# RWKV-7 and pooling trunk: the chunk solves take both heads through one block-diagonal operand, with right-hand sides of 64 columns

## The chip, the cores and the metric

The program runs on one core of a Trainium2 chip. The metric is the device time of one execution in microseconds (us); lower is better. A core has a matrix engine (PE, with its weight loads shown apart as PEld), a vector engine (DVE), a scalar engine (ACT), a general engine (POOL) and queues that issue DMAs (SP among them). Each engine takes its instructions in order.

## The reference

The model has one layer (DEPTH = 1), T = 512 tokens, D = 2048. The part that matters here is the RWKV-7 group: 16 heads of 64 channels, each with a state S of 64x64 that is updated token by token:

```python
h = rms_norm(x, norm_g[i])
z = h @ w_in[i]          # r, k, v, decay, rate | rwkv gate | pool input | pool gate
# per head, per token t:
sa = S @ (-kk_t)
S  = S * w_t + sa (kk_t * a_t)^T + v_t k_t^T
y_t = S @ r_t
```

Beside it stand a pooling group, the gates, an output projection and a last gated embedding; each of these is a dense product with large weights.

## The kernel before

Everything that is dense (the projections `z`, later the output and the gate) is done in three passes on PE (`mm3`), each a 128x512 matmul on operands split into a high and a low part. A weight tile arrives as `raw`, ACT casts it to `whi` (L132), DVE subtracts to get `wlo` (L133).

The recurrence is done in chunks of C = 64 tokens (NCH = 8), for a pair j of heads at a time (NJ = 8 pairs; a pair fills 128 partitions). For each pair:

- `scores(j)` forms the products of keys and rates inside a chunk and masks them into `mt` (L630).
- `invert(j)` inverts the 32x32 triangular blocks row by row on DVE (31 steps, `tm` L657 and `xw` L661), writes the result to memory (`xd`) and loads it as the blocks on the diagonal of `x1`, a tile of 8 units x 64 columns that POOL zeroes for every pair.
- `gather(j)` builds the 32x32 block off the diagonal of each inverse: transposes `y1` on DVE (L734), 16 small matmuls `pq` (L739), copies `q` on ACT (L745), 16 small matmuls `px` (L748), copies into `x1` on ACT (L752).
- `recur(j)` is the chain over the 8 chunks. In each chunk: `py` on PE (the state's part); `zs` on DVE (L787) adds `mv` to it; `pu` on PE (L793) is the solve, the inverse times `zs`; `uv` are two copies on ACT (L797); `ps` on PE is the state's update; `sbd` are two operations on DVE (L807, L809) that write the next state.

Before, `zs` is 128x128 and holds the right-hand sides of both heads side by side in one half of its partitions, zeros in the other. `pu` multiplies by `x1` of both heads (128 columns), so its 128x128 result holds four 64x64 blocks, of which the two on the diagonal are used.

PE takes its instructions in the order of the program. Between the steps of the chain the program pumps filler, matmuls of the dense projections: 6 between `py` and `pu`, 9 between `pu` and `ps`, 9 after `ps` (`HC = (6, 9, 9)`), and others between the bursts of `gather` (`H1 = 6` matmuls each). As long as DVE and ACT are done within this filler, PE does not wait. The order on DVE, ACT, POOL and SP is made by a scheduler at build time from its own estimate of durations; `zs`, `sbd` and `uv` have a raised priority there (`HP`). `step()` lets three rows of the next pair's inversion through after the operation in `lead[0]`.

Of the kernel before, what the change touches and what calls it, by code (L numbers as in the profile page):

```python
# [9 lines left out]
F32 = mybir.dt.float32  # L10
# [3 lines left out]
ALU = mybir.AluOpType  # L14

P = 128
# [5 lines left out]
NJ = DR // P  # L22
LORA = 64
C = 64
# [10 lines left out]
def trunk_kernel(ctx: ExitStack, tc: tile.TileContext, x, p, norm_g, w_in, mu, w0, w_up, a0, a_up,  # L35
# [329 lines left out]
    for t_ in sbd + zsp:  # L365
# [243 lines left out]
    def scores(j):  # L609
        ar, bk, v_ = (st_[j][n_] for n_ in ("ar", "bk", "v_"))  # L610
        kph, kpl = st_[j].pop("kp")

        ps = psM.tile([P, T], F32, name=f"pbo{j}", tag="m")
        mm(ps, blk, kph, start=True, stop=False)
        mm(ps, blk, kpl, start=False, stop=True)
        bv = rw.tile([P, T], F32, name=f"bv{j}", tag="bv", bufs=2)
        nc.vector.tensor_tensor(bv, ps, v_, ALU.mult)

        mt = rw.tile([P, 2, 8, 2, C], F32, name=f"mt{j}", tag="mt", bufs=2)
        pm = [[psM.tile([P, T], F32, name=f"pm{j}_{par}0", tag="m"),  # L620
               psY.tile([P, T], F32, name=f"pm{j}_{par}1", tag="y")] for par in range(2)]
        for par in range(2):
            for q in range(4):
                for h in range(2):
                    rows = slice(64 * h, 64 * h + 64)
                    mm(pm[par][h][:, q * P:(q + 1) * P], bk[rows, q, 2 * par:2 * par + 2, :],
                       ar[rows, q, 2 * par:2 * par + 2, :], start=True, stop=True)
        for par in range(2):
            for h in range(2):
                nc.vector.tensor_tensor(mt[:, par, h::2, :, :],  # L630
                                        pm[par][h].rearrange("p (u a t) -> p u a t", u=4, a=2),
                                        msk[:, par:par + 2, :].unsqueeze(1).to_broadcast([P, 4, 2, C]), ALU.mult)

        nd = dram.tile([2, 2, 8, 32, 32], F32, name=f"nd{j}", tag="nd")
        for par in range(2):
            pb = 64 * (1 - par)
            for b in range(2):
                rows = slice(pb + 32 * b, pb + 32 * b + 32)
                nc.sync.dma_start(out=nd[par, b].rearrange("u r c -> r u c"),
                                  in_=mt[rows, par, :, 1 - par, 32 * b:32 * b + 32])  # L640
        nb = []
        for i in range(2):
            t_ = rw.tile([P, 16, 32], F32, name=f"n32{j}_{i}", tag=("kk", "kp")[i])
            nc.sync.dma_start(out=t_, in_=nd[:, :, :, 16 * i:16 * i + 16, :].rearrange(
                "a b u r c -> (a b u) r c").unsqueeze(0).to_broadcast([4, 32, 16, 32]))
            nb.append(t_)
        st_[j].update(mt=mt, nb=nb, bv=bv)


    def invert(j):  # L650
        nb = st_[j].pop("nb")
        xw = rw.tile([P, 8, 32], F32, name=f"xw{j}", tag="xw")
        tm = rw.tile([P, 8, 32], F32, name=f"tm{j}", tag="tm")
        for s in range(31):
            n_, w_ = s // 4 + 1, 31 - s
            xin = i32 if s == 0 else xw
            nc.vector.tensor_tensor(tm[:, 0:n_, 0:w_], xin[:, 0:n_, s:s + 1].to_broadcast([P, n_, w_]),  # L657
                                    nb[s // 16][:, s % 16:s % 16 + 1, s + 1:32].to_broadcast([P, n_, w_]), ALU.mult)
            if s == 0:
                nc.gpsimd.tensor_copy(xw, i32)  # L660
            nc.vector.tensor_tensor(xw[:, 0:n_, s + 1:32], xw[:, 0:n_, s + 1:32], tm[:, 0:n_, 0:w_], ALU.add)  # L661
            yield
        xd = dram.tile([2, 2, 8, 8, 4, 32], F32, name=f"xd{j}", tag="xd")
        for q in range(4):
            nc.sync.dma_start(out=xd[:, :, :, :, q, :].rearrange("a b u i c -> (a b u) i c"),
                              in_=xw[32 * q:32 * q + 32])
        x1 = rw.tile([P, 8, C], F32, name=f"x1{j}", tag="x1", bufs=2)
        nc.gpsimd.memset(x1, 0.0)
        for par in range(2):
            pb = 64 * (1 - par)  # L670
            for b in range(2):
                nc.sync.dma_start(out=x1[pb + 32 * b:pb + 32 * b + 32, :, 32 * b:32 * b + 32],
                                  in_=xd[par, b].rearrange("u i q c -> (i q) u c"))

        st_[j]["x1"] = x1


    def gather(j):
# [25 lines left out]
        ps = psM.tile([P, 8, C], F32, name=f"pmv{j}", tag="m")  # L704
        for u in range(8):
            for par in range(2):
                pb, kb = 64 * (1 - par), 64 * par
                h = u % 2
                mm(ps[pb:pb + 64, u, :], mt[kb:kb + 64, par, u, 1 - par, :],
                   uv[kb:kb + 64, 2 * (u // 2) + par, 64 * h:64 * h + 64], start=True, stop=True)  # L710
        mv = rw.tile([P, 4, P], F32, name=f"mv{j}", tag="mv")
        nc.scalar.copy(zsp[0][64:128, :].rearrange("p (h t) -> p h t", h=2), ps[64:128, 0:2, :])
        nc.scalar.copy(mv.rearrange("p q (h t) -> p (q h) t", h=2), ps)

        d.update(uv=uv, bkn=bkn, mv=mv)
# [4 lines left out]
            pending.pop()()  # L720
        pump(HX)

        x1 = d["x1"]

        def units(fn):
            for u in range(8):
                for par in range(2):
                    fn(u, par, 64 * (1 - par))

        y1 = rw.tile([P, 8, 32], F32, name=f"y1{j}", tag="tm")  # L730

        with tc.issue_after(late[0].ins):
            for pb in (0, 64):
                yt = nc.vector.transpose(y1[pb:pb + 32], x1[pb:pb + 32, :, 0:32])  # L734
# [4 lines left out]
        units(lambda u, par, pb: mm(ps3[pb + 32:pb + 64, u, :],  # L739
                                                  mt[pb:pb + 32, par, u, 1 - par, 32:64],  # L740
                                                  y1[pb:pb + 32, u, :], start=True, stop=True,
                                                  tile_position=(pb, pb + 32)))
        q2t = rw.tile([P, 8, 32], F32, name=f"q2{j}", tag="xw")
        for pb in (0, 64):
            nc.scalar.copy(q2t[pb + 32:pb + 64], ps3[pb + 32:pb + 64])  # L745
        pump(H1)
        ps4 = psM.tile([P, 8, 32], F32, name=f"px2{j}", tag="m")
        units(lambda u, par, pb: mm(ps4[pb:pb + 32, u, :], q2t[pb + 32:pb + 64, u, :],  # L748
                                                  x1[pb + 32:pb + 64, u, 32:64], start=True, stop=True,
                                                  tile_position=(pb + 32, pb)))  # L750
        for pb in (0, 64):
            nc.scalar.copy(x1[pb:pb + 32, :, 32:64], ps4[pb:pb + 32])  # L752
        pump(H1)


    def recur(j, work, between):
        d = st_.pop(j)
        pw, ar, mt, bv, uv, bkn, mv, x1 = (d[n_] for n_ in ("pw", "ar", "mt", "bv", "uv", "bkn", "mv", "x1"))
        hop = [0]
        HC1, HC2, HC3 = HC  # L760
        lead = [None]
# [12 lines left out]
        for ch in range(NCH):  # L774
# [8 lines left out]
            if ch > 0:  # L783
                mm(py[:, sl], ar[:, q, 2 * par:2 * par + 2, :], cur, start=ch in (1, 4), stop=True,
                                 skip_group_check=True)
                with tc.high_priority(offset=HP):
                    lead[0] = nc.vector.tensor_tensor(zs[pb:pb + 64], py[pb:pb + 64, sl], mv[pb:pb + 64, q, :],  # L787
                                                      ALU.add)
                step()
                pump(HC1)  # L790

            psu = psS.tile([P, T], F32, name=f"pu{j}_{ch}", tag="s")
            mm(psu[:, 0:P], x1[:, 2 * q:2 * q + 2, :], zs, start=True, stop=True)  # L793
            for h in range(2):
                hc = slice(64 * h, 64 * h + 64)
                with tc.high_priority(offset=HP):
                    nc.scalar.copy(uv[pb:pb + 64, ch, hc], psu[hc, hc])  # L797
            step()
            pump(HC2)
            if ch < NCH - 1:  # L800
# [16 lines left out]
            if ch % 4 == 3:  # L817
                for qq in range(2):
                    for h in range(2):
                        for pr in range(2):  # L820
                            c_ = ch - 3 + 2 * qq + pr
                            yr = slice(64 * pr, 64 * pr + 64)
                            o_ = (2 * qq + pr) * P + 64 * h
                            mm(py[yr, o_:o_ + 64], mt[:, pr, 2 * (c_ // 2) + h, pr, :],
                                             uv[:, c_, 64 * h:64 * h + 64], start=False, stop=True,
                                             skip_group_check=True)
                py4 = py.rearrange("p (s c) -> p s c", c=P)
# [8 lines left out]

        for _ in work:
            pass


        st = rw.tile([P, 8, 6], F32, name=f"st{j}", tag="st")
# [41 lines left out]
    pump(H2)  # L883
    for _ in invert(0):
        pass
    pump(HT)
    gather(0)
    for j in range(NJ):
# [278 lines left out]
```

## Time and profile before

| | |
|---|---|
| median of 3 runs | 1102.54 us (1102.44 to 1103.41) |
| profiled execution | 1103.22 us |
| its span (first to last instruction) | 1101.5 us |
| granted PE clock, mean | 0.997 |
| PE busy | 1074.0 us (98%) |
| DVE busy | 708.1 us (64%) |
| ACT busy | 448.8 us (41%) |
| POOL busy | 77.7 us (7%) |

A row of a group reads: line, engine, operation, out<-in, partitions x elements and type, count, then busy time, mean ns of one, then the engine's idle time just before and what ended most of it. A row of the timeline reads: start in us from the start of the span, duration in us, engine, line, operation, out<-in, count, and in brackets the idle time before it with what ended that. PE's matmuls are pipelined, so a 128x512 matmul is recorded with about 0.39 us while the next one starts 0.23 us after it. A row of stretches has, after the stretch and its length, the busy time of PE, PEld, DVE, ACT and POOL, the granted clock, the DMA share and GB/s.

### The profile page before, as it was taken

The page shows a single profiled execution, that of the slowest core. Times are in us where ns is not written, and L with a number is a line of the kernel's source. Part 1 is how long each engine was busy: PE and PEld are TensorE (multiplying, and loading weights), DVE is VectorE, ACT ScalarE, POOL GpSimd, SP SyncE. Part 2 cuts the span into 40 slices and gives each one's busy share as a digit, 9 for nine tenths or more (in the row PEclk, how much of TensorE's full clock was granted, in tenths as well). Part 3 has the DMA queues.
Part 4 walks back from the last instruction along what each step waited for, and adds up shares of the span by engine and source line. Part 5 has one row for each costly group of instructions (what it writes and reads, how often), then busy time and mean ns, then how long its engine had stood idle before and what let it go on. Part 6 is the DMA issues. An engine that isn't in the chain of part 4 may idle for free.

```text
span 1101.5 us, 17252 instructions
## 1 busy us (share of the span) xinstructions
PE 1074.0 (98%) x6090; PEld 878.4 (80%) x6090; DVE 708.1 (64%) x1835; ACT 448.8 (41%) x917; POOL 77.7 (7%) x180
## 2 busy tenths in 40 slices
PE   5999999999999999999999999999999999999996
PEld 4888887887877878877878788788888888888885
DVE  6687868878688589687786866454433424445366
ACT  7633535334335245353343344543222222233247
POOL 2100110110110101101101101000000000000000
PEclk9999999999999999999999999999999999999998
DMA  7433433332423333333334242775534438455344
GB/s 231 117 94 97 110 97 83 97 94 73 133 75 101 109 86 86 99 78 96 86 86 124 77 138 95 231 239 162 167 127 137 166 100 254 132 181 163 124 134 153
DMA packets 178485, 138.56 MB, mean 126 GB/s; under 512 B 34677, under 2 KB 139742, under 8 KB 178398
## 3 DMA queue, kind: packets, MB, share of 16 engines
q1 hardware_dynamic: 157694, 103.89, 32.1%
q10 hardware_dynamic: 20704, 33.56, 9.6%
q8 instruction: 48, 0.79, 0.3%
q14 instruction: 39, 0.32, 0.1%
HBM read 118.02 MB, written 18.87 MB: 124 GB/s over the span
## 4 chain that ended last, share of the span: by engine, by line
PE 67%; DVE 4%; ACT 3%; DMA 1%; issue 1%; ACTq 0%; DVEq 0%
PE acc_o L157 16%; PE acc_g L157 13%; PE zb L157 13%; PE zg L157 5%; PE zk L157 4%; PE zr L157 4%; PE zv L157 2%; PE py L157 2%; PE pu L157 1%; PE pp L157 1%; PE pm L157 1%; PE pple L157 1%; DMA pled<-ple 1%; PE ps L157 1%; DVE xw L661 1%
## 5 line engine op out<-in xcount | busy, mean ns | idle before, releaser
L133 DVE TENSOR_TENSOR wlo_g<-raw_g,whi_g 128x512 fp32r<-128x512 f32 x88 | 59.6, 686 | 88.4 <-ACT whi_g L132 88.3
L157 PE MATMUL zb<-hhi,whi_b 128*128 128x512 f32 x256 | 107.0, 418 | 0.0
L133 DVE TENSOR_TENSOR wlo_o<-raw_o,whi_o 128x512 fp32r<-128x512 f32 x64 | 43.8, 690 | 90.3 <-ACT whi_o L132 90.3
L157 PE MATMUL zb<-hhi,wlo_b 128*128 128x512 f32 x256 | 100.5, 392 | 0.0
L132 ACT CAST whi_g<-raw_g 128x512 fp32r<-128x512 f32 x88 | 54.4, 621 | 112.8 <-PE acc_g L157 69.9
L157 PE MATMUL acc_o<-whi_o,ylo 128*128 128x512 f32 x256 | 100.2, 391 | 0.0
L157 PE MATMUL zb<-hlo,whi_b 128*128 128x512 f32 x256 | 99.9, 390 | 0.0
L157 PE MATMUL acc_o<-whi_o,yhi 128*128 128x512 f32 x256 | 99.9, 390 | 0.0
L157 PE MATMUL acc_o<-wlo_o,yhi 128*128 128x512 f32 x256 | 99.7, 390 | 0.0
L157 PE MATMUL acc_g<-whi_g,x2hi 128*128 128x512 f32 (+1 forms) x224 | 86.7, 387 | 0.0
L157 PE MATMUL acc_g<-wlo_g,x2hi 128*128 128x512 f32 (+1 forms) x224 | 86.4, 386 | 0.0
L157 PE MATMUL acc_g<-whi_g,x2lo 128*128 128x512 f32 x224 | 86.0, 385 | 0.0
L132 ACT CAST whi_o<-raw_o 128x512 fp32r<-128x512 f32 x64 | 39.8, 624 | 95.6 <-PE acc_o L157 95.6
L816 POOL TENSOR_SCALAR s0p<-sbd,pw 64x64 f32<-64x64 f32 x96 | 55.9, 582 | 322.8 <-DVE sbd L809 256.4
L132 ACT CAST whi_b<-raw_b 128x512 fp32r<-128x512 f32 x64 | 39.8, 621 | 85.7 <-PE zv L157 34.2
L133 DVE TENSOR_TENSOR wlo_b<-raw_b,whi_b 128x512 fp32r<-128x512 f32 x64 | 43.7, 685 | 33.6 <-ACT whi_b L132 33.3
L157 PEld LDWEIGHTS zb<-hhi,wlo_b 128*128 128x128 f32 x256 | 48.0, 188 | 11.1
L661 DVE TENSOR_TENSOR xw<-xw,tm 128x60 f32<-128x60 f32 (+24 forms) x248 | 52.0, 210 | 7.0
L157 PEld LDWEIGHTS acc_o<-wlo_o,yhi 128*128 128x128 f32 x256 | 48.1, 188 | 10.0
L157 PEld LDWEIGHTS acc_o<-whi_o,ylo 128*128 128x128 f32 x256 | 48.1, 188 | 9.8
L157 PEld LDWEIGHTS acc_o<-whi_o,yhi 128*128 128x128 f32 x256 | 48.1, 188 | 9.7
L157 PEld LDWEIGHTS zb<-hhi,whi_b 128*128 128x128 f32 x256 | 48.3, 188 | 8.5
(283 smaller groups left out, 2543.2 us busy)
## 6 DMA issues: line engine op xcount, KB each, us to landing
raw_b<-in_w_in_dram SPq DMA_DIRECT2D x64, 256.0 KB
raw_o<-in_w_out_dram SPq DMA_DIRECT2D x64, 256.0 KB
raw_g<-in_w_pg_dram SPq DMA_DIRECT2D x64, 256.0 KB
raw_k<-in_w_in_dram SPq DMA_DIRECT2D x32, 256.0 KB
raw_r<-in_w_in_dram SPq DMA_DIRECT2D x32, 256.0 KB
raw_v<-in_w_in_dram SPq DMA_DIRECT2D x32, 256.0 KB
raw_g<-in_w_in_dram SPq DMA_DIRECT2D x32, 256.0 KB
n<-nd SPq DMA_DIRECT2D x16, 256.0 KB
```

The lines of the kernel that those rows point to most:

```text
L132: nc.scalar.copy(hi, raw)
L133: nc.vector.tensor_tensor(lo, raw, hi.bitcast(F32), ALU.subtract)
L157: i = nc.tensor.matmul(*a, **k)
L661: nc.vector.tensor_tensor(xw[:, 0:n_, s + 1:32], xw[:, 0:n_, s + 1:32], tm[:, 0:n_, 0:w_], ALU.add)
L816: nc.gpsimd.tensor_scalar(s0p[hc, :], nxt[hc, hc], pcn[hc], None, ALU.mult)
```

## The change

The inverses of both heads go on the diagonal of one 128x128 operand per chunk. `xdg` (8 chunks x 128 columns) is one tile for all pairs, zeroed once; each pair overwrites the blocks on the diagonal. `zs` is 128x64: one head's right-hand side in the upper 64 partitions, the other's in the lower. `side(par, h)` tells which half a head has in a chunk. So `pu` moves 64 columns instead of 128 and its 128x64 result is used whole. The two halves of `zs` are now written by two adds of 64x64 instead of one of 64x128, and `lead[0]` is the second of them. The four DMAs that load the inverse (`inverse_rows`) come after the pair's recurrence in the program, since `xdg` is still read by it. The index of `mt` is (par ^ h, chunk), the DMAs through `nd` and `xd` are re-indexed to it in the same number and size. In `gather` the transposes are 4 of 32x(4x32) instead of 2 of 32x256, and so are the copies `q`; the small matmuls run chunk by chunk and head by head, which puts four in a row on one 32x32 place of the array where there were two. The first `zs` is copied in two parts.

```diff
-    zsp = [rw.tile([P, P], F32, name=f"zs{i}") for i in range(2)]
+    zsp = [rw.tile([P, C], F32, name=f"zs{i}") for i in range(2)]
+    xdg = rw.tile([P, NCH, P], F32, name="xdg")
...
+    def side(par, h):
+        return 64 * (1 - (par ^ h))
...
-        x1 = rw.tile([P, 8, C], F32, name=f"x1{j}", tag="x1", bufs=2)
-        nc.gpsimd.memset(x1, 0.0)
...
+    def inverse_rows(j):
+        xd = st_[j].pop("xd")
+        for e in range(2):
             for b in range(2):
-                nc.sync.dma_start(out=x1[pb + 32 * b:pb + 32 * b + 32, :, 32 * b:32 * b + 32],
-                                  in_=xd[par, b].rearrange("u i q c -> (i q) u c"))
+                rc_ = slice(64 * (1 - e) + 32 * b, 64 * (1 - e) + 32 * b + 32)
+                nc.sync.dma_start(out=xdg[rc_, :, rc_], in_=xd[b, e].rearrange("u i q c -> (i q) u c"))
...
         def units(fn):
-            for u in range(8):
-                for par in range(2):
-                    fn(u, par, 64 * (1 - par))
+            for ch in range(NCH):
+                for h in range(2):
+                    fn(ch, 2 * (ch // 2) + h, ch % 2, h, 64 * (1 - ch % 2), side(ch % 2, h))
...
-        for pb in (0, 64):
-            nc.scalar.copy(q2t[pb + 32:pb + 64], ps3[pb + 32:pb + 64])
+        for par in range(2):
+            pb = 64 * (1 - par)
+            for h in range(2):
+                sd = side(par, h)
+                nc.scalar.copy(q2t[sd + 32:sd + 64, par::2, :], ps3[pb + 32:pb + 64, h::2, :])
...
-                with tc.high_priority(offset=HP):
-                    lead[0] = nc.vector.tensor_tensor(zs[pb:pb + 64], py[pb:pb + 64, sl], mv[pb:pb + 64, q, :],
-                                                      ALU.add)
+                for h in range(2):
+                    sd, hc = side(par, h), slice(64 * h, 64 * h + 64)
+                    with tc.high_priority(offset=HP):
+                        lead[0] = nc.vector.tensor_tensor(zs[sd:sd + 64], py[pb:pb + 64, sl][:, hc],
+                                                          mv[pb:pb + 64, q, hc], ALU.add)
...
-            mm(psu[:, 0:P], x1[:, 2 * q:2 * q + 2, :], zs, start=True, stop=True)
+            mm(psu[:, 0:C], xdg[:, ch, :], zs, start=True, stop=True)
             for h in range(2):
-                hc = slice(64 * h, 64 * h + 64)
+                sd, hc = side(par, h), slice(64 * h, 64 * h + 64)
                 with tc.high_priority(offset=HP):
-                    nc.scalar.copy(uv[pb:pb + 64, ch, hc], psu[hc, hc])
+                    nc.scalar.copy(uv[pb:pb + 64, ch, hc], psu[sd:sd + 64, 0:C])
...
         for _ in work:
             pass
+        if j + 1 < NJ:
+            inverse_rows(j + 1)
```

The scheduler places the new operations. On DVE, in the recurrence of pair 3 at its first chunks (`wlo_k` and `wlo_r` are parts of weight tiles, `sg` belongs to the gate), the order before was:

```order
L787 TENSOR_TENSOR zs_569<-py_0_4568,mv_4382 64x128
L133 TENSOR_TENSOR wlo_k_3_2558<-raw_k_3_2555,whi_k_3_2557 128x512
L374 SCALAR_TENSOR_TENSOR sg_4696<-sg_4696,zg_4502 128x512
L133 TENSOR_TENSOR wlo_r_0_2564<-raw_r_0_2561,whi_r_0_2563 128x512
L809 SCALAR_TENSOR_TENSOR sbd_566<-ps_1_4743,pw_3343,s0p_0_4598 64x64 x2
L787 TENSOR_TENSOR zs_568<-py_0_4568,mv_4382 64x128
```

and with the change it is:

```order
L803 TENSOR_TENSOR zs_569<-py_0_4601,mv_4410 64x64
L133 TENSOR_TENSOR wlo_k_3_2571<-raw_k_3_2568,whi_k_3_2570 128x512
L803 TENSOR_TENSOR zs_569<-py_0_4601,mv_4410 64x64
L381 SCALAR_TENSOR_TENSOR sg_4730<-sg_4730,zg_4535 128x512
L133 TENSOR_TENSOR wlo_r_0_2577<-raw_r_0_2574,whi_r_0_2576 128x512
L825 SCALAR_TENSOR_TENSOR sbd_566<-ps_1_4777,pw_3361,s0p_0_4631 64x64 x2
```

The `wlo` that stood behind the add now stands between its two halves.

Further on in the same recurrence, at chunk 5, where DVE also has the rows of the next inversion (`tm`, `xw`), the order before was:

```order
L661 TENSOR_TENSOR xw_4848<-xw_4848,tm_4849 128x4x17
L787 TENSOR_TENSOR zs_569<-py_4_4910,mv_4382 64x128
L133 TENSOR_TENSOR wlo_v_3_2761<-raw_v_3_2758,whi_v_3_2760 128x512
L657 TENSOR_TENSOR tm_4849<-xw_4848,n_0_4666 128x4x16
L370 SCALAR_TENSOR_TENSOR sr_4992<-zr_4825,prm,sr_4992 128x511
```

and with the change it is:

```order
L669 TENSOR_TENSOR xw_4884<-xw_4884,tm_4885 128x4x17
L803 TENSOR_TENSOR zs_569<-py_4_4946,mv_4410 64x64
L133 TENSOR_TENSOR wlo_v_3_2775<-raw_v_3_2772,whi_v_3_2774 128x512
L803 TENSOR_TENSOR zs_569<-py_4_4946,mv_4410 64x64
L665 TENSOR_TENSOR tm_4885<-xw_4884,n_0_4699 128x4x16
```

Again the `wlo` has come between the halves. This holds for 18 of the 56 pairs of adds: all seven of pair 3, all seven of pair 5, one of pair 1 (chunk 7) and three of pair 7 (chunk 4 with one `wlo_e`, chunks 5 and 6 with two each). In the other 38 the halves stand next to each other.

On ACT, in the `gather` of pair 0 (`kph` is a cast, `uv` the first chunk's copies), the order before was:

```order
L369 ACTIVATE sv_1546<-zv_1375,dprm 128x512
L745 COPY q_1593<-pq_1576 32x256 x2
L132 CAST whi_g_0_1156<-raw_g_0_1154 128x512
L137 CAST kph_1656<-kp_1649 128x512
L752 COPY x_1142<-px_1614 32x8x32 x2
```

and with the change it is:

```order
L376 ACTIVATE sv_1545<-zv_1373,dprm 128x512
L759 COPY q_1594<-pq_1577 32x4x32 x3
L132 CAST whi_g_0_1154<-raw_g_0_1152 128x512
L759 COPY q_1594<-pq_1577 32x4x32
L137 CAST kph_1659<-kp_1652 128x512
L766 COPY xdg<-px_1617 32x8x32 x2
```

The cast of a weight tile now stands ahead of the last of the four copies. So it is for pairs 0, 1, 3, 5 and 7; for pairs 2, 4 and 6 the four copies stand together.

More of the change, by code (lines that the diff above doesn't have):

```diff
@@ L364, in trunk_kernel @@
     nc.gpsimd.memset(uaz[1][0:64, :].bitcast(F32), 0.0)
-    for t_ in sbd + zsp:
+    for t_ in sbd + [xdg]:
         nc.gpsimd.memset(t_, 0.0)
+    def side(par, h):
+        return 64 * (1 - (par ^ h))
     def shifted(ps, dst, mi):
@@ L629, in scores @@
             for h in range(2):
-                nc.vector.tensor_tensor(mt[:, par, h::2, :, :],
+                nc.vector.tensor_tensor(mt[:, par ^ h, par::2, :, :],
                                         pm[par][h].rearrange("p (u a t) -> p u a t", u=4, a=2),
                                         msk[:, par:par + 2, :].unsqueeze(1).to_broadcast([P, 4, 2, C]), ALU.mult)
-        nd = dram.tile([2, 2, 8, 32, 32], F32, name=f"nd{j}", tag="nd")
+        nd = dram.tile([2, 16, 32, 32], F32, name=f"nd{j}", tag="nd")
         for par in range(2):
@@ L638, in scores @@
                 rows = slice(pb + 32 * b, pb + 32 * b + 32)
-                nc.sync.dma_start(out=nd[par, b].rearrange("u r c -> r u c"),
-                                  in_=mt[rows, par, :, 1 - par, 32 * b:32 * b + 32])
+                nc.sync.dma_start(out=nd[b, par::2].rearrange("u r c -> r u c"),
+                                  in_=mt.rearrange("p e u a t -> p (e u) a t")[rows, par::2, 1 - par,
+                                                                               32 * b:32 * b + 32])
         nb = []
@@ L706, in gather @@
             for par in range(2):
-                pb, kb = 64 * (1 - par), 64 * par
-                h = u % 2
-                mm(ps[pb:pb + 64, u, :], mt[kb:kb + 64, par, u, 1 - par, :],
+                pb, kb, h = 64 * (1 - par), 64 * par, u % 2
+                mm(ps[pb:pb + 64, u, :], mt[kb:kb + 64, par ^ h, 2 * (u // 2) + par, 1 - par, :],
                    uv[kb:kb + 64, 2 * (u // 2) + par, 64 * h:64 * h + 64], start=True, stop=True)
         mv = rw.tile([P, 4, P], F32, name=f"mv{j}", tag="mv")
-        nc.scalar.copy(zsp[0][64:128, :].rearrange("p (h t) -> p h t", h=2), ps[64:128, 0:2, :])
+        for h in range(2):
+            nc.scalar.copy(zsp[0][side(0, h):side(0, h) + 64, :], ps[64:128, h, :])
         nc.scalar.copy(mv.rearrange("p q (h t) -> p (q h) t", h=2), ps)
@@ L721, in gather @@
         pump(HX)
-        x1 = d["x1"]
+        x1 = xdg
         def units(fn):
-            for u in range(8):
-                for par in range(2):
-                    fn(u, par, 64 * (1 - par))
+            for ch in range(NCH):
+                for h in range(2):
+                    fn(ch, 2 * (ch // 2) + h, ch % 2, h, 64 * (1 - ch % 2), side(ch % 2, h))
         y1 = rw.tile([P, 8, 32], F32, name=f"y1{j}", tag="tm")
         with tc.issue_after(late[0].ins):
-            for pb in (0, 64):
-                yt = nc.vector.transpose(y1[pb:pb + 32], x1[pb:pb + 32, :, 0:32])
+            for par in range(2):
+                pb = 64 * (1 - par)
+                for h in range(2):
+                    sd = side(par, h)
+                    yt = nc.vector.transpose(y1[pb:pb + 32, h::2, :], x1[sd:sd + 32, par::2, sd:sd + 32])
         if j + 1 < NJ:
@@ L738, in gather @@
         ps3 = psM.tile([P, 8, 32], F32, name=f"pq2{j}", tag="m")
[L739 to L742, printed above, removed]
+        units(lambda ch, u, par, h, pb, sd: mm(ps3[pb + 32:pb + 64, u, :],
+                                               mt[pb:pb + 32, par ^ h, ch, 1 - par, 32:64],
+                                               y1[pb:pb + 32, u, :], start=True, stop=True,
+                                               tile_position=(pb, pb + 32)))
         q2t = rw.tile([P, 8, 32], F32, name=f"q2{j}", tag="xw")
-        for pb in (0, 64):
-            nc.scalar.copy(q2t[pb + 32:pb + 64], ps3[pb + 32:pb + 64])
+        for par in range(2):
+            pb = 64 * (1 - par)
+            for h in range(2):
+                sd = side(par, h)
+                nc.scalar.copy(q2t[sd + 32:sd + 64, par::2, :], ps3[pb + 32:pb + 64, h::2, :])
         pump(H1)
         ps4 = psM.tile([P, 8, 32], F32, name=f"px2{j}", tag="m")
-        units(lambda u, par, pb: mm(ps4[pb:pb + 32, u, :], q2t[pb + 32:pb + 64, u, :],
-                                                  x1[pb + 32:pb + 64, u, 32:64], start=True, stop=True,
-                                                  tile_position=(pb + 32, pb)))
+        units(lambda ch, u, par, h, pb, sd: mm(ps4[sd:sd + 32, ch, :], q2t[sd + 32:sd + 64, ch, :],
+                                               x1[sd + 32:sd + 64, ch, sd + 32:sd + 64], start=True, stop=True,
+                                               tile_position=(sd + 32, sd)))
         for pb in (0, 64):
-            nc.scalar.copy(x1[pb:pb + 32, :, 32:64], ps4[pb:pb + 32])
+            nc.scalar.copy(x1[pb:pb + 32, :, pb + 32:pb + 64], ps4[pb:pb + 32])
         pump(H1)
@@ L757, in recur @@
         d = st_.pop(j)
-        pw, ar, mt, bv, uv, bkn, mv, x1 = (d[n_] for n_ in ("pw", "ar", "mt", "bv", "uv", "bkn", "mv", "x1"))
+        pw, ar, mt, bv, uv, bkn, mv = (d[n_] for n_ in ("pw", "ar", "mt", "bv", "uv", "bkn", "mv"))
         hop = [0]
@@ L885, in trunk_kernel @@
         pass
+    inverse_rows(0)
     pump(HT)
```

10 lines of the change are left out of this document (5 added, 5 removed).

## The prediction

> **What bounds the kernel now.** I read the busy shares and the chain of waits first, then the groups by line, the waits of PE, and last the single chunks in the timeline.
>
> ```profile
> PE 1074.0 (98%) x6090; PEld 878.4 (80%) x6090; DVE 708.1 (64%) x1835; ACT 448.8 (41%) x917; POOL 77.7 (7%) x180
> PE 67%; DVE 4%; ACT 3%; DMA 1%; issue 1%; ACTq 0%; DVEq 0%
> ```
>
> PE is busy for 98% and two thirds of the chain that ended last are PE. So time goes only where PE's own work grows or shrinks, or where PE starts to wait. The 64% of DVE is an average over unlike stretches. Two stretches of 20 us in the recurrence of pair 3 (length, then PE, PEld, DVE, ACT, POOL busy):
>
> ```profile
> 366.00:386.00 20.00, 20.00 (x111) 16.64 (x110) 10.94 (x38) 7.52 (x17) 2.67 (x6) 1.00 0.38 108
> 386.00:406.00 20.00, 19.82 (x95) 15.93 (x93) 18.06 (x69) 7.39 (x16) 2.02 (x5) 1.00 0.27 80
> ```
>
> In the second DVE works 18.06 of 20 us, and PE is 0.18 us short of full: there DVE has almost nothing to spare.
>
> The groups that the change touches, or that price its parts, and the one wait that stands between DVE and the solve (idle us, times, largest):
>
> ```profile
> L157 PE MATMUL pu<-zs,x 128*128 128x128 f32 x128 | 25.7, 282 | 1.2 <-DVE zs L787 1.1
> L787 DVE TENSOR_TENSOR zs<-py,mv 64x128 f32<-64x128 f32 x56 | 16.1, 287 | 21.6 <-PE py L157 20.6
> L661 DVE TENSOR_TENSOR xw<-xw,tm 128x64 f32<-128x64 f32 x8 | 1.8, 222 | 0.2
> L133 DVE TENSOR_TENSOR wlo_r<-raw_r,whi_r 128x512 fp32r<-128x512 f32 x32 | 22.0, 688 | 17.3 <-ACT whi_r L132 17.0
> L797 ACT COPY uv<-pu 64x64 f32<-64x64 f32 x128 | 26.6, 208 | 43.9 <-PE pu L157 42.9
> L745 ACT COPY q<-pq 32x256 f32<-32x256 f32 x16 | 5.8, 365 | 11.7 <-PE pq L157 9.9 <-issue 1.7
> L734 DVE STREAM_TRANSPOSE y<-x 32x256 f32<-32x256 f32 x16 | 6.9, 429 | 0.2
> PEld pu L157 <- DVE zs L787: 5.6, 11, 0.8
> ```
>
> There are 64 solves, each recorded as two passes (128). The wait for `zs` now holds 11 of them up, by at most 0.8 us.
>
> **Term 1: the solves move 64 columns instead of 128.** What a solve takes from PE is seen between two fillers:
>
> ```profile
> 145.67 0.39 PE L157 MATMUL zg<-hhi,wlo_g 128*128 128x512 f32 x1
> 145.90 0.38 PE L157 MATMUL pu<-zs,x 128*128 128x128 f32 x2
> 146.04 0.48 PE L157 MATMUL zg<-hhi,whi_g 128*128 128x512 f32 x1
> 146.35 0.40 PE L157 MATMUL zg<-hlo,whi_g 128*128 128x512 f32 x1
> 146.59 0.40 PE L157 MATMUL zg<-hhi,wlo_g 128*128 128x512 f32 x1
> ```
>
> From 145.67 to 146.35 there are two fillers, at 0.23 us each, and the pair of passes: 0.68 - 0.46 = 0.22 us, 0.11 us a pass. If the columns that are moved set these 0.11 us, half would go: 128 x 0.055 = 7.0 us. If the load of the 128 weight columns sets them, nothing goes, since the weights stay 128x128 and each pass has its own load. Two kinds of rows bear on it. The first filler after a change of the array's tiling shows what a load that isn't hidden costs, and the smaller solves show passes with fewer columns on both sides (min/median/max in ns):
>
> ```profile
> 123.04 0.50 PE L157 MATMUL zb<-hhi,whi_b 128*128 128x512 f32 x1
> L157 PE MATMUL pq<-y,mt x256: 191/191/212, 122.4 to 652.4; 32*32 32x32 f32 x128
> L157 PE MATMUL py<-uv,mt x256: 222/222/270, 154.7 to 705.3; 128*64 128x64 f32 x128
> ```
>
> The filler takes 0.50 instead of 0.39: 0.11 us for 128 weight columns, just what a pass of `pu` takes. The largest of `pq` is 21 ns above its median with 32 weight columns, that of `py` 48 ns with 64: again about 0.8 ns a column. The moved columns change with the weights in these rows, so they don't exclude the other reading, but the load alone already fills the 0.11 us. I take -0.2 us; ends 0 and -7.0.
>
> The Trainium skill, "TensorE: Matmul & The Clock Gate", section "Back-to-back issue gap", gives an isolated matmul 134 cycles for 128 moved columns and about 60 for 64 or fewer; at its 2.4 GHz that is an estimate of 31 ns a pass, -4.0 us in all, by which the sum below would be +3.5 instead of +7.3. The same page, section "LDWEIGHTS (loading the stationary operand)", counts the weights' columns alone, 107 ns for 128 by its formula, which is the trace's 0.11 us and speaks against one. No run shown here has 128 weight columns with 64 moved.
>
> **Term 2: two adds on DVE for one, and what has come between them.** A 64x64 add has no row; the nearest is the 128x64 one, 222 ns. Two are 0.44 us where one was 0.287: +0.16 us in each of 56 chunks. `pu` needs both. In 18 chunks the scheduler has put a `wlo` of 0.69 us between the halves, so there `zs` comes 0.85 us later. That costs time where DVE's slack is smaller. A solve that isn't held up starts 0.23 us after its last filler; a held one 0.06 us after `zs` (recurrence 1, chunk 7: 253.47 + 0.28 + 0.06 = 253.81):
>
> ```profile
> 253.08 0.40 PE L157 MATMUL zv<-hhi,wlo_v 128*128 128x512 f32 x1
> 253.81 0.38 PE L157 MATMUL pu<-zs,x 128*128 128x128 f32 x1 [0.33 <-DVE zs L787]
> 253.47 0.28 DVE L787 TENSOR_TENSOR zs<-py,mv 64x128 f32<-64x128 f32 x1
> ```
>
> This solve was due at 253.31 and already comes 0.5 us late; a `wlo_b` now comes in between: up to 0.85 more. I take +0.9 with what earlier chunks have shifted.
>
> Recurrence 3, all seven split. An early chunk and three late ones:
>
> ```profile
> 372.85 0.69 DVE L133 TENSOR_TENSOR wlo_r<-raw_r,whi_r 128x512 fp32r<-128x512 f32 x1
> 373.71 0.38 PE L157 MATMUL pu<-zs,x 128*128 128x128 f32 x2
> 392.61 0.28 DVE L787 TENSOR_TENSOR zs<-py,mv 64x128 f32<-64x128 f32 x1
> 393.16 0.38 PE L157 MATMUL pu<-zs,x 128*128 128x128 f32 x2
> 399.14 0.40 PE L157 MATMUL zv<-hhi,wlo_v 128*128 128x512 f32 x1
> 399.71 0.38 PE L157 MATMUL pu<-zs,x 128*128 128x128 f32 x1 [0.18 <-DVE zs L787]
> 405.67 0.28 DVE L787 TENSOR_TENSOR zs<-py,mv 64x128 f32<-64x128 f32 x1
> 406.14 0.38 PE L157 MATMUL pu<-zs,x 128*128 128x128 f32 x2
> ```
>
> Chunk 2: the `wlo` ends at 373.54, the second half 0.22 later, the solve starts at 373.82 instead of 373.71: 0.1 late, and about as much in the other early chunks, +0.3. Chunk 5: 392.61 + 0.28 + 0.85 + 0.06 = 393.80 instead of 393.16: 0.6 late. Chunk 6 already starts 0.33 late (due at 399.37). Chunk 7: 406.01 would do, 406.14 is when it starts, slack 0.13. Where DVE is full, these do not add: a late PE gives DVE the same time back. What remains is the lateness of the last chunk, one split and three added 0.16 less the slack: 0.69 + 0.48 - 0.13 = 1.0, to 1.2 with the backlog that chunk 6 already has. So recurrence 3 is +1.4. Recurrence 5 is built alike, all seven split; +1.5.
>
> Recurrence 7, chunk 5, where two `wlo_e` come between:
>
> ```profile
> 688.19 0.69 DVE L133 TENSOR_TENSOR wlo_e<-raw_e,whi_e 128x512 fp32r<-128x512 f32 x1 [0.31 <-ACT whi_e L132]
> 689.72 0.68 DVE L133 TENSOR_TENSOR wlo_e<-raw_e,whi_e 128x512 fp32r<-128x512 f32 x1
> 689.63 0.38 PE L157 MATMUL pu<-zs,x 128*128 128x128 f32 x2
> ```
>
> The first can't start before its `whi_e` at 688.19; the second follows at 688.88 or, at the latest, at 689.72. So the second half ends between 689.79 and 690.62 and the solve is 0.2 to 1.0 late. Chunk 6 is alike, chunks 4 and 7 lose about 0.1 and 0.2: +1.5. The chunks with adjacent halves in recurrences 0, 2, 4 and 6 pay at most their 0.16, and only where the 0.16 meets no slack: +0.7.
>
> Sum of term 2: 0.9 + 1.4 + 1.5 + 1.5 + 0.7 = +6.0 us. Low end +2.0, if only the late chunks pay their own 0.16 (11 that wait now) and single splits are absorbed; high end +12, if all 18 splits cost 0.69 in full without any being given back. Behind a late `pu` on PE stand its 9 fillers and all that follows: PE is in order, so each wait goes into the end.
>
> **Term 3: four copies `q` for two.** By the rows for 64 and 256 elements (`uv` 0.208, `q` 0.365 us) a copy of 128 is about 0.26: 1.04 us instead of 0.74. For pairs 0, 1, 3, 5 and 7 a weight cast of 0.62 us now stands ahead of the last copy.
>
> ```profile
> 123.20 0.74 ACT L745 COPY q<-pq 32x256 f32<-32x256 f32 x2 [1.73 <-issue]
> 123.97 0.62 ACT L132 CAST whi_g<-raw_g 128x512 fp32r<-128x512 f32 x1
> 124.62 0.47 PE L157 MATMUL px<-x,q 32*32 32x32 f32 x17
> ```
>
> 123.20 + 1.04 + 0.62 = 124.86, against `px` at 124.62: 0.3 late. Six fillers lie between for pairs 0, 1 and 5, twelve for 3 and 7: 3 x 0.3 = +1.0; ends 0 and +1.5.
>
> **Term 4: the order of the 32x32 matmuls.** Sixteen bursts (`pq` and `px` of eight pairs) look like this one:
>
> ```profile
> 196.83 0.69 PE L157 MATMUL pq<-y,mt 32*32 32x32 f32 x32
> ```
>
> 32 passes, 22 ns each, alternate between two places of the array by twos; now by fours. If passes at one place don't overlap, a burst could grow by up to 0.2 us: +3.2. Nothing in the row shows such a dependence: I take +0.5, ends 0 and +3.2.
>
> **What costs nothing.** `xdg` is a single tile, so its loads wait for the last `pu` of the pair. The smallest gap there:
>
> ```profile
> 329.89 0.38 PE L157 MATMUL pu<-zs,x 128*128 128x128 f32 x2
> 334.32 1.81 SPq L672 DMA_DIRECT2D x<-xd  x4
> ```
>
> The solve is over 4.1 us before SP issues the load, so SP's queue waits for nothing new; behind it stand only weight loads. The eight memsets that POOL loses lie on an engine busy for 7%. The split copy of the first `zs` has the 26 fillers (13 + 13, 6 us) between it and `pu`. The two added transposes (0.43 us for 256 elements; four for 128 take about 0.3 us more than two) have the 13 fillers ahead of `pq`. If that cover went, each would cost its 0.3 us a pair, 2.4 us.
>
> **The sum.** -0.2 + 6.0 + 1.0 + 0.5 = +7.3 us. The profiled execution took 1103.22 us, 1.7 more than its span and 0.7 more than the median; the difference is carried to the median: 1102.54 + 7.3 = 1110 us.
>
> **The rivals.** (a) Faster: the passes follow the moved columns, -7.0 us. Then the added waits decide: under 4.8 us in all it is faster by over 0.2% (2.2 us, about what a measurement here can tell from no change). With the low ends it is 1102.5 - 7.0 + 2.0 + 0.5 = 1098 us, with my waits 1103.0. For it speaks that no row has 64 moved columns on 128 weight columns; against it that the weight load alone explains 0.11 us. (b) No change that shows: DVE catches up, since the waits give back the splits, and the low ends hold: +2.0, 1104.5 us. For it speaks that the wait for `zs` is only 5.6 us in all now; against it the 18.06 of 20 us. (c) Slower still: every split is paid and the four-in-a-row order costs: +12 + 1.5 + 1 = 1117 us.
>
> **Chances.** My forecast (1105 to 1114) 0.60; (a) 0.10, of which half ends faster; (b) 0.13; (c) 0.17. Range 1103 to 1117. Faster by over 0.2% 0.06, within 0.2% 0.12, slower by over 0.2% 0.82.
>
> **What would show it.** Right: `pu` takes 0.22 us between fillers as before; PE's wait for `zs` grows from 5.6 to some 11 to 13 us, with recurrences 3, 5 and 7 first, and a `wlo` in the timeline between two halves just ahead of each wait. Wrong: a solve between fillers of 0.11 us (term 1), a `zs` wait that stays at 5 us (term 2), a 64x64 add near 0.29 us, `px` that starts on time, bursts of 0.9 us.

## The result, and the profile after

The changed kernel takes 1114.93 us (median of 4, 1114.10 to 1116.12) against 1102.95 us before (median of 4, 1102.44 to 1103.41): ratio 1.0108, 95% interval 1.0096 to 1.0120, +12.0 us. Its profiled execution took 1114.47 us with a span of 1112.7 us, 11.2 us longer than before; the granted clock is 0.998.

The busy line, and the two stretches of recurrence 3 that answer to those shown of before (its first solve now comes 2.5 us later, its last 4.8 us):

```profile
PE 1079.3 (97%) x6090; PEld 878.6 (79%) x6090; DVE 723.2 (65%) x1907; ACT 450.1 (40%) x941; POOL 74.0 (7%) x171
...
368.00:388.00 20.00, 19.99 (x108) 15.90 (x107) 11.00 (x37) 6.78 (x16) 2.67 (x6) 1.00 0.38 107
388.00:408.00 20.00, 18.82 (x90) 14.87 (x89) 17.67 (x68) 6.58 (x15) 1.96 (x4) 1.00 0.24 69
```

In the late stretch PE is now idle for 1.2 of 20 us where it was 0.2, with fewer instructions done (90 for 95). The groups, and PE's waits for `zs` (us, times, longest):

```profile
L157 PE MATMUL pu<-zs,xdg 128*128 128x64 f32 x128 | 23.8, 267 | 7.8 <-DVE zs L803 7.4
L803 DVE TENSOR_TENSOR zs<-py,mv 64x64 f32<-64x64 f32 x112 | 24.8, 221 | 24.2 <-PE py L157 22.3
L759 ACT COPY q<-pq 32x128 f32<-32x128 f32 x32 | 8.3, 258 | 12.4 <-PE pq L157 10.0 <-issue 1.8
PE pu L157 <- DVE zs L803: 7.4, 14, 1.0
PEld pu L157 <- DVE zs L803: 0.9, 3, 0.3
```

A 64x64 add takes 0.221 us and a copy of 128 elements 0.258, as sized. The idle time in a row of waits begins only when PE and its weight loads have run dry. I use a fuller measure: how much later than 0.229 us after its last filler each solve starts (56 solves; the first of each recurrence, whose `zs` is copied, is left out). Lateness in us by recurrence:

| recurrence | 0 | 1 | 2 | 3 | 4 | 5 | 6 | 7 | sum |
|---|---|---|---|---|---|---|---|---|---|
| before | 0.40 | 0.69 | 0.06 | 0.37 | 0.18 | 0.30 | 0.55 | 0.32 | 2.85 |
| after | 0.76 | 1.78 | 0.66 | 2.45 | 0.22 | 2.33 | 0.91 | 3.23 | 12.35 |

So 9.5 of the 11.2 us are solves that wait for `zs`. Chunk 5 of recurrence 3, on DVE and on PE:

```profile
395.93 0.22 DVE L803 TENSOR_TENSOR zs<-py,mv 64x64 f32<-64x64 f32 x1
396.07 0.67 DVE L133 TENSOR_TENSOR wlo_v<-raw_v,whi_v 128x512 fp32r<-128x512 f32 x1
396.78 0.22 DVE L803 TENSOR_TENSOR zs<-py,mv 64x64 f32<-64x64 f32 x1
396.19 0.40 PE L157 MATMUL zv<-hhi,wlo_v 128*128 128x512 f32 x1
397.14 0.41 PE L157 MATMUL pu<-zs,xdg 128*128 128x64 f32 x2 [0.56 <-DVE zs L803]
```

The first half is done at 396.15, the solve is due at 396.42, the `wlo` keeps the second half back until 396.78, it is done at 397.00, and the solve starts at 397.14: 0.7 us late. Before, this solve was on time.

One more thing stands in these rows. The solve starts 0.14 us after the second half is done, where the prediction's row of before (253.47 + 0.28 to 253.81) has 0.06. This is so throughout: before, all 10 solves that come over 0.02 us late start 0.055 us after the add has ended; now 29 of the 32 such solves start 0.148 us after the second add. In the trace those 29 have a separate semaphore instruction of 0.05 us on PE's queue between the add and the weight load; the other 3, and the 10 of before, have none and start after 0.055 us.

What the change meant to shorten, the solve between two fillers, is unchanged:

```profile
146.53 0.39 PE L157 MATMUL zg<-hhi,wlo_g 128*128 128x512 f32 x1
146.76 0.33 PE L157 MATMUL pu<-zs,xdg 128*128 128x64 f32 x2
146.90 0.47 PE L157 MATMUL zg<-hhi,whi_g 128*128 128x512 f32 x1
147.22 0.39 PE L157 MATMUL zg<-hlo,whi_g 128*128 128x512 f32 x1
```

From 146.53 to 147.22 is 0.69 us, two fillers and 0.23; before it was 0.68. Over all 64 solves the smallest such addition is 0.220 us in both kernels. The second pass of a solve and the weight loads beside it, first before, then now, show where the halved columns go:

```profile
145.90 0.19 PEld L157 LDWEIGHTS pu<-zs,x 128*128 128x128 f32 x1
146.01 0.28 PE L157 MATMUL pu<-zs,x 128*128 128x128 f32 x1
146.01 0.19 PEld L157 LDWEIGHTS zg<-hhi,whi_g 128*128 128x128 f32 x1
...
146.77 0.19 PEld L157 LDWEIGHTS pu<-zs,xdg 128*128 128x128 f32 x1
146.82 0.27 PE L157 MATMUL pu<-zs,xdg 128*128 128x64 f32 x1
146.87 0.19 PEld L157 LDWEIGHTS zg<-hhi,whi_g 128*128 128x128 f32 x1
```

The second pass does start earlier behind the first one: 0.055 us (29 of the 30 solves that are on time) where it was 0.108. But the load of the next filler still starts 0.108 to 0.110 us after the load of the second pass, in all 64 solves of both kernels, and the filler starts 0.03 us after its load. So the filler comes 0.084 us after the second pass where it was 0.031, and what the columns save is gone.

The fourth copy `q` of pair 0, behind the cast on ACT, and what it does to the `px` burst:

```profile
123.44 0.82 ACT L759 COPY q<-pq 32x128 f32<-32x128 f32 x3 [1.75 <-issue]
124.29 0.62 ACT L132 CAST whi_g<-raw_g 128x512 fp32r<-128x512 f32 x1
124.93 0.25 ACT L759 COPY q<-pq 32x128 f32<-32x128 f32 x1
124.87 1.00 PE L157 MATMUL px<-xdg,q 32*32 32x32 f32 x32
```

The burst starts on time and stops in its middle for the last copy: 1.00 us instead of 0.69, and 0.96 in pairs 1 and 5.

### The profile page after: what moved, and what is told of

Its sections match the earlier page's. It is cut to its first block, busy times and chain, and to the rows that moved or that the text cites. A ratio compares the mean times of both kernels' runs of the same rounds, so it can differ in the third digit from the quotient of the medians.

```text
span 1112.7 us, 17373 instructions
## 1 busy us (share of the span) xinstructions
PE 1079.3 (97%) x6090; PEld 878.6 (79%) x6090; DVE 723.2 (65%) x1907; ACT 450.1 (40%) x941; POOL 74.0 (7%) x171
```

## The experiments

Theory A: the loss is PE waiting for the second half of `zs`, mostly because a `wlo` stands between the halves. Rival B: the longer pair of adds alone, wherever the `wlo` stands. Rival C: the new operand and what comes with it.

**1. The adds adjacent.** One edit to the changed kernel:

```diff
-                    with tc.high_priority(offset=HP):
+                    with tc.high_priority(offset=100 * HP):
                         lead[0] = nc.vector.tensor_tensor(zs[sd:sd + 64], py[pb:pb + 64, sl][:, hc],
```

> The changed kernel with one edit: the two adds of zs get so high a priority that they stand next to each other on DVE in all 56 chunks (in the changed kernel a weight split wlo stands between them in 18). Theory A (the loss is PE waiting for the second half of zs; the split chunks make up 7.8 of the 12.4 us of these waits, against 1.2 us in the same chunks before): the waits for zs fall from 12.4 to 5 to 7 us, the time to 1108 to 1110 us, ratio to before 1.004 to 1.007. Rival B (the loss is the longer pair of adds itself, +0.16 us in each chunk, and DVE's backlog, wherever wlo stands): the waits stay over 10 us, the time over 1112. Rival C (the loss comes from the new operand, its loads or the copies around it): no change, 1114 to 1115.

Measured 1109.53 us (median of 5), ratio to before 1.0060 (1.0048 to 1.0073). The lateness of the solves falls from 12.35 to 6.32 us (by recurrence 0.73, 1.18, 0.65, 1.29, 0.22, 1.18, 0.90, 0.16). Chunk 5 of recurrence 3, and the wait:

```profile
393.84 0.45 DVE L803 TENSOR_TENSOR zs<-py,mv 64x64 f32<-64x64 f32 x2
394.31 0.69 DVE L133 TENSOR_TENSOR wlo_v<-raw_v,whi_v 128x512 fp32r<-128x512 f32 x1
393.99 0.40 PE L157 MATMUL zv<-hhi,wlo_v 128*128 128x512 f32 x1
394.43 0.41 PE L157 MATMUL pu<-zs,xdg 128*128 128x64 f32 x2
...
PE pu L157 <- DVE zs L803: 3.3, 8, 0.6
```

0.2 late instead of 0.7. Theory A holds for 5.2 us of the loss in the times (12.0 less 6.8, each against the kernel before as it was measured beside it), 6.0 in the lateness, as expected. B alone falls, but it has a part: 6.32 is still 3.5 over before. Of these 3.5, some 1.5 are the 0.09 us by which a late solve starts later behind its adds than before (an estimate, added up over the 18 late solves that show it). The time is 6.8 us over before, more than that: the edit also moved the last pair's normalization on DVE behind a wait for a weight cast, and `pyt`, the transposes of that pair's result, which stand between fillers too, now wait:

```profile
717.73 0.39 PE L157 MATMUL zb<-hhi,wlo_b 128*128 128x512 f32 x1
719.21 0.77 PE L161 MATMUL pyt<-ident,ysb 128*128 128x128 f32 x2 [1.09 <-DVE ysb L872]
720.20 0.69 PE L161 MATMUL pyt<-ident,ysb 128*128 128x128 f32 x2 [0.21 <-DVE ysb L872]
```

This group of four transposes adds 2.77 us to the fillers where the median one adds 0.45; the same group adds 1.38 in the kernel before and in the changed one. So some 1.4 us of the 6.8 come from the edit's own reordering.

**2. Two adds in the kernel before.** Nothing of the new operand:

```diff
-                with tc.high_priority(offset=HP):
-                    lead[0] = nc.vector.tensor_tensor(zs[pb:pb + 64], py[pb:pb + 64, sl], mv[pb:pb + 64, q, :],
-                                                      ALU.add)
+                for h in range(2):
+                    hc = slice(64 * h, 64 * h + 64)
+                    with tc.high_priority(offset=HP):
+                        lead[0] = nc.vector.tensor_tensor(zs[pb:pb + 64, hc], py[pb:pb + 64, sl][:, hc],
+                                                          mv[pb:pb + 64, q, hc], ALU.add)
```

> The kernel before with one edit: its add of zs (64x128) is written as two adds of 64x64 on the same partitions. Solve, operand, copies and DMAs stay as before; the scheduler puts a wlo between the halves in 18 chunks here too. Theory A: this alone makes most of the loss, waits for zs 11 to 13 us instead of 2.9, time 1110 to 1113 us. Rival C (the new operand and what comes with it): 1102 to 1104 us.

Measured 1107.90 us (median of 5), ratio 1.0047 (1.0035 to 1.0060): a loss of 5.2 us, less than the expected 1110 to 1113, and above C's 1102 to 1104. Lateness 8.38 us, below the expected 11 to 13 (0.74, 1.49, 0.25, 1.82, 0.15, 2.14, 0.57, 1.23). The same chunk:

```profile
393.45 0.22 DVE L789 TENSOR_TENSOR zs<-py,mv 64x64 f32<-64x64 f32 x1
393.59 0.67 DVE L133 TENSOR_TENSOR wlo_v<-raw_v,whi_v 128x512 fp32r<-128x512 f32 x1
394.19 0.21 DVE L789 TENSOR_TENSOR zs<-py,mv 64x64 f32<-64x64 f32 x1
393.70 0.40 PE L157 MATMUL zv<-hhi,wlo_v 128*128 128x512 f32 x1
394.54 0.46 PE L157 MATMUL pu<-zs,x 128*128 128x128 f32 x2 [0.45 <-DVE tm L657]
```

The wait is there without the new operand (its row names `tm`, which ran when the solve started; what the solve needs is the half that ended at 394.40). So the split add makes 5.5 us of lateness and 5.2 of the 12.0 us of loss by itself; late solves here too start 0.145 us after the second half, so the longer way from add to solve comes with the two adds and not with the new operand. Why the queue has one more wait there is not shown. The remaining 6.8 us come with the rest of the change: of the 6.9 us between the two spans 5.1 stand at the solves and 1.0 at the bursts of `px` and `pq`. The other 4.0 us of lateness between this kernel and the changed one (12.35 less 8.38): 2.0 lie in recurrence 7, where the scheduler here puts the `wlo` between the halves of chunks 3, 4 and 7 and leaves 5 and 6 together. The other 2.0 are spread over recurrences 1, 2, 3, 5 and 6 and are not settled one by one; a part is the 0.1 us told in the last section.

**3. The copies `q` together.** The first experiment's kernel with this edit:

```diff
-                nc.scalar.copy(q2t[sd + 32:sd + 64, par::2, :], ps3[pb + 32:pb + 64, h::2, :])
+                with tc.high_priority(offset=100 * HP):
+                    nc.scalar.copy(q2t[sd + 32:sd + 64, par::2, :], ps3[pb + 32:pb + 64, h::2, :])
```

> The first experiment's kernel, and the four copies q of each gather stand together on ACT, so that no weight cast comes ahead of the fourth. If the cast is why px is interrupted (px bursts of 0.95 to 0.99 us in pairs 0, 1 and 5, 0.69 in the others), all px bursts are 0.69 us and the time is 0.8 us under the first experiment. If the four copies by themselves are too long, the bursts stay above 0.9 us. Against the kernel before 1107 to 1109 us by theory A.

```profile
123.11 1.11 ACT L760 COPY q<-pq 32x128 f32<-32x128 f32 x4 [1.75 <-issue]
124.24 0.62 ACT L132 CAST whi_g<-raw_g 128x512 fp32r<-128x512 f32 x1
124.54 0.69 PE L157 MATMUL px<-xdg,q 32*32 32x32 f32 x32
```

All eight bursts are 0.69 us, so the cast ahead of the fourth copy was the cause, and four copies of 1.11 us fit. The 0.8 us did not come back in the time: 1109.20 against 1109.53 us, spans of 1107.4 us both. The runs of each spread over 2 us, so this is unclear rather than shown to be nothing. In the trace 0.4 us of it come back at the first solves of pairs 0, 1 and 5, which now add 0.41, 0.35 and 0.30 us to the fillers for 0.23, 0.23 and 0.22.

**4. The operands exchanged.** In the changed kernel, whose copies `uv` then read the product at its new place; this product is not the solve, so the kernel leaves the solve out:

```diff
-            mm(psu[:, 0:C], xdg[:, ch, :], zs, start=True, stop=True)
+            mm(psu[0:C, 0:P], zs, xdg[:, ch, :], start=True, stop=True)
```

> The changed kernel with the operands of the solve exchanged: zs is the stationary side (64 weight columns), xdg moves with 128 columns; the product is then another one than the solve. One look, for what a pair of passes takes between two fillers where nothing waits (0.22 us before with 128 weight and 128 moved columns, and 0.22 us in the changed kernel with 128 and 64). If the load of the weight columns sets a pass: 0.16 to 0.18 us (one load of 64 columns, one of the filler's 128). If a pass cannot be shorter whatever its operands: 0.22 us. The time follows by some 3 us at most, plus or minus what DVE makes of it.

Neither: 1125.6 us (one run), and the pair takes far longer.

```profile
147.26 0.40 PE L157 MATMUL zg<-hhi,wlo_g 128*128 128x512 f32 x1
147.59 0.43 PE L157 MATMUL pu<-xdg,zs 128*64 128x128 f32 x2
147.95 0.50 PE L157 MATMUL zg<-hhi,whi_g 128*128 128x512 f32 x1
148.28 0.39 PE L157 MATMUL zg<-hlo,whi_g 128*128 128x512 f32 x1
```

From 147.26 to 148.28 are 1.02 us, two fillers and 0.56, in place of 0.22. The solve starts 0.33 after its filler instead of 0.23, and the next filler takes 0.50: with 64 weight columns the array is in another form (128*64 in the row, 128*128 in the fillers), and the loads on both sides of that change are no longer hidden: the load of the solve starts with it at 147.59 and that of the next filler at 147.95, where in the changed kernel they start 0.23 and 0.03 us ahead. The run says what a change of form costs in a chain between fillers, 0.34 us, and leaves the question it was made for open.

**5 and 6. The inversion's rows spread out.** One line in the kernel before, and the same in the third experiment's kernel:

```diff
-    HS, HN = 9, 3
+    HS, HN = 6, 2
```

> The kernel before with one edit: the rows of the next pair's inversion go in twos from the 7th step of the chain on (HS, HN = 6, 2) instead of in threes from the 10th, so that DVE has about 12 instead of 18 instructions of it in each of the late chunks; the work is the same. Theory A (solves wait because DVE is full in the late chunks, with zs behind the inversion's rows): the waits for zs in chunks 5 to 7 fall from 2.8 to under 1 us, those of py for sbd (1 to 2 us in all) too, the time to 1099 to 1101 us. Rival B (it is the number of instructions on DVE, wherever they stand): 1102 to 1103 us.

> The third experiment's kernel (adds of zs adjacent, copies q together) with the same edit as the run above, HS, HN = 6, 2. Theory A: the 6.3 us of waits for zs that are left there lie in chunks 5 to 7 and fall under 2 us; time 1103 to 1106 us, 4 to 5 us under the third experiment, and still 2 us or more above the kernel before with the same edit, since px waits and the adds are longer. Rival B: 1108 to 1110 us, as the third experiment.

The kernel before with this edit takes 1099.47 us (median of 7), ratio 0.9974 (0.9962 to 0.9985): it beats both kernels. Lateness 1.35 us instead of 2.85, and 0.02 us or less in each of recurrences 1 to 5.

```profile
383.00:403.00 20.00, 20.00 (x99) 16.67 (x98) 16.04 (x55) 7.89 (x17) 2.01 (x5) 1.00 0.28 81
...
389.77 0.28 DVE L787 TENSOR_TENSOR zs<-py,mv 64x128 f32<-64x128 f32 x1 [0.35 <-PE py L157]
390.72 0.39 PE L157 MATMUL zv<-hhi,wlo_v 128*128 128x512 f32 x1
390.96 0.38 PE L157 MATMUL pu<-zs,x 128*128 128x128 f32 x2
...
PEld pu L157 <- DVE zs L787: 2.0, 3, 0.8
```

In the late stretch DVE now has 16.04 instead of 18.06 us of work, PE is full, and the add waits for `py` again instead of for DVE. Theory A: it is where DVE's work stands, not how much of it there is.

In the third experiment's kernel the edit brings 1103.38 us (median of 11) from 1109.20, ratio to before 1.0008 (0.9999 to 1.0016): it cannot be told from the kernel before. Lateness 1.78 us. So with the halves adjacent and room on DVE the solves are nearly on time. That the time is level with the kernel before is in part a gain which that kernel can have as well: against it with the same edit 3.9 us of the 12.0 remain. Of these 1.4 are again the last pair's `pyt` (2.76 us) and 0.4 lateness; the rest is not broken down.

**7. Twice the columns.** In the kernel before, the solve moves `zs` twice, 256 columns:

```diff
-            mm(psu[:, 0:P], x1[:, 2 * q:2 * q + 2, :], zs, start=True, stop=True)
+            mm(psu[:, 0:2 * P].rearrange('p (a c) -> p a c', a=2), x1[:, 2 * q:2 * q + 2, :],
+               zs.unsqueeze(1).to_broadcast([P, 2, P]), start=True, stop=True)
```

> The kernel before, its solve moving 256 columns (zs twice) instead of 128 against the same 128 weight columns; the second half of the product is not used. One look, for what a pair of passes takes between two fillers where nothing waits. If the weight loads set 0.11 us a pass and the columns pass beside them at the fillers' rate (512 in 0.229 us): 256 columns are 0.115 us, so the pair takes 0.22 to 0.24 us. If 128 columns already took a whole pass of 0.11 us, 256 take 0.22 us a pass, 0.44 us the pair. Time: by the first 1103 to 1105 us, by the second 1116 to 1118.

```profile
145.68 0.39 PE L157 MATMUL zg<-hhi,wlo_g 128*128 128x512 f32 x1
145.91 0.59 PE L157 MATMUL pu<-zs,x 128*128 128x256 f32 x2
146.16 0.59 PE L157 MATMUL zg<-hhi,whi_g 128*128 128x512 f32 x1
146.58 0.40 PE L157 MATMUL zg<-hlo,whi_g 128*128 128x512 f32 x1
```

From 145.68 to 146.58 are 0.90 us, two fillers and 0.44: the second expectation. Moving 128 columns in this f32 form already takes 0.11 us a pass, about half the fillers' speed (fp32r operands, 512 columns in 0.229). So with 128 columns the moved columns filled the pass, and yet halving them in the changed kernel gained nothing: something else, with the same 0.11 us, is behind it. The rows of the weight loads in the section on the result name it: with 64 moved columns the two passes stand 0.055 us apart, but the loads still follow each other by 0.108 us, and the next filler waits for its own. No run here has 64 moved columns behind a shorter load in the same form of the array. Time 1114.14 us (one run), 2 us under the 1116 to 1118.

## Why the prediction was right, and where its terms were off

The range, the direction and the mechanism held: the solves gained nothing, and PE waits for the second half of `zs`. The size was forecast too low. The measured 1114.93 us is 5 us over the forecast of 1110, just above the 1105 to 1114 that was given the largest chance, and nearer to the 1117 of rival (c), which is the end of the range. The steps, each against the trace:

- Term 1 (-0.2 us): 0, the smallest solve between fillers takes 0.220 us in both kernels. The reason given was half of it: the weights' load is not alone at 0.11 us, the 128 moved columns were there too (experiment 7). With 64 the load is left as the limit, as the rows of the loads show, and rival (a) fell. The two small rows read beside it give 21 ns for 32 weight columns and 48 ns for 64, which is 0.66 and 0.75 ns a column and only roughly the 0.8 that was read.
- Term 2 (+6.0 us): 9.5, mis-sized. Recurrence by recurrence, forecast and measured: 1: 0.9 and 1.1; 3: 1.4 and 2.1; 5: 1.5 and 2.0; 7: 1.5 and 2.9; 0, 2, 4 and 6: 0.7 and 1.4. The step that was wrong is "Where DVE is full, these do not add: a late PE gives DVE the same time back." In recurrence 3 the late chunks 5, 6 and 7 start 0.73, 0.78 and 0.43 late, 1.9 together, and each has to be paid anew. From one `zs` to the next DVE is busy there for 6.0 to 6.5 of 6.7 to 7.1 us, about as long as the 6.2 us that a chunk takes on PE where nothing is late, so the time that PE loses goes to DVE's next instructions and not to an earlier `zs`; this last step is argued, and experiments 5 and 6, where DVE has less work in these chunks and most of the waits go, bear it out. The early chunks lose 0.06 to 0.18 each. In recurrence 7 chunks 3, 5, 6 and 7 are 0.65, 0.95, 0.77 and 0.58 late: chunk 3 has no `wlo` between its halves and was not counted, but the `wlo_e` that followed the add before now stands ahead of both halves (from 684.02; the halves follow at 684.74); chunk 5 came to the upper of its two bounds (0.2 to 1.0).
- A second size in term 2: "a held one 0.06 us after `zs`" became 0.148 us. The forecast for chunk 5 of recurrence 3, 0.64 late, is off by just this 0.09. Over the 29 late solves that show it, it comes to 2.6 of the 9.5 us; that is an estimate from the trace, since no run takes this wait away alone.
- A late solve costs PE some more than it is late, since its own loads are no longer hidden: from 397.14 to 397.67 in the changed kernel solve and filler take 0.53 us, from 146.76 to 147.22 on time 0.46. All 64 solves take 11.4 us more between the fillers than before, 9.5 of it the lateness of the table, 0.3 lateness at the first chunks.
- Term 3 (+1.0 us): bursts of 1.00, 0.96 and 0.96 us for 0.69, +0.8, by the cast as forecast. Yet `px` starts on time, which the prediction had named as a sign of being wrong: the delay came in the middle of the burst, not ahead of it.
- Term 4 (+0.5 us): `pq` bursts 0.71 for 0.69 us, `px` without change, +0.2 in all.
- At nothing: no wait in the profile is put down to the new loads of `xdg`. The longer gather makes the first solve of pairs 0 and 4 0.3 us late together.

Against these stands a gain: 1.4 us less at `py`, where PE waits less for `sbd`. Together that is 11.0 of the 11.2 us between the spans. Of the rivals, (c), every split paid, was nearest.

One sign that the prediction named did not come in its form: the rows of waits for `zs` hold 7.4 and 0.9 us, not 11 to 13. They count only the time in which PE has run dry; by lateness it is 12.35.

## What to carry to other kernels

Count an edit that cuts an operand in half on the engine that makes the operand as well: two instructions for one give the scheduler a place between them, and what it puts there is paid nearly in full where that engine is full (0.7 to 0.8 us late for a `wlo` of 0.69 at chunks 5 and 6 of recurrence 3). Read the slack in the stretch, not in the average: DVE's 64% hid chunks with about 90%. And where a wait is found, look first for work that can stand elsewhere: spreading the inversion's rows gained 3.3 us with one pair of numbers.

## What the runs showed of the hardware that was not expected

- A 128x128 f32 pass between fillers takes 0.11 us with 64 and with 128 moved columns and 0.22 with 256. With 64 the two passes of a solve are 0.055 us apart, but their weight loads and the next filler's keep 0.108 us from start to start; a change of the array's form from 128*128 to 128*64 and back costs 0.34 us around one pair.
- A solve that waits for `zs` starts 0.055 us after the add where its weight load waits for it directly, and 0.148 us after it where PE's queue has one more semaphore instruction in between (29 of 32 late solves in the changed kernel, none of 10 before).
- On DVE the second half of an add starts 0.07 to 0.08 us before the `wlo` ahead of it has ended where it reads and writes the partitions from 0 on, and 0.03 us after it otherwise. Odd chunk 3 of recurrence 3, first the changed kernel, whose second half writes from partition 64:

```profile
381.78 0.69 DVE L133 TENSOR_TENSOR wlo_r<-raw_r,whi_r 128x512 fp32r<-128x512 f32 x1
...
382.50 0.22 DVE L803 TENSOR_TENSOR zs<-py,mv 64x64 f32<-64x64 f32 x1
```

then the kernel before with two adds, where both halves lie from partition 0:

```profile
379.44 0.69 DVE L133 TENSOR_TENSOR wlo_r<-raw_r,whi_r 128x512 fp32r<-128x512 f32 x1
...
380.05 0.21 DVE L789 TENSOR_TENSOR zs<-py,mv 64x64 f32<-64x64 f32 x1
```

This is so in all 11 split odd chunks of the latter and in none of the 18 split second halves of the former.
